# Input projections of a hybrid decoder step: how the first tiles are loaded and split, and when a bias table is spread

## The chip, the cores and the metric

The kernel runs on one core of a Trainium2 chip. The metric is the device time of one execution in microseconds (us). Three runs of the kernel before gave a median of 2597.31 us. The engines are named as in the profile: PE (TensorE matmul; PEld is its weight load), DVE (VectorE), ACT (ScalarE), POOL (GpSimd) and SP (SyncE, which issues most DMAs here). Each works through its own list of instructions in order and waits on semaphores for the others.

## The reference

One layer of a decoder step for a prompt of 2048 positions and for 8 samples of 4 positions, which share the weights. All data is float32.

```python
z = rmsnorm(x, norm1_g) @ w_in            # (2048 + 32) x 1024 @ 1024 x 2560
q, k, v, u, g = split(z, 5)               # 512 columns each
# attention, 8 heads of 64, three dilated branches, relative-position bias, merged
s = q . k / 8 + bias[branch][head, j]     # j: distance 0, d, 2d, ... within the window
# gating: g is layer-normed, multiplied with a causal 128 x 128 matrix per group, times u
x = x + concat(att, u * gate) @ w_out
x = x + (silu(h @ w_gate) * (h @ w_up)) @ w_down      # h = rmsnorm(x, norm2_g), 2816 wide
y = rmsnorm(x, final_g)
```

`rmsnorm` needs the mean of the squares of each row of x. The samples attend over a cache of 2048 keys and values each. The bias is a table lookup by distance; a Toeplitz matrix of it is needed for each head.

## The kernel before

A float32 product is made of three products in a reduced format: each operand is split into a high part (`xh`, `wh`) and a low part (`xl`, `wl`), and PE adds high·high, high·low and low·high (L318 to L320). The high part is a copy on ACT (L135 for x, L220 for weights), the low part a subtraction on DVE or POOL (L138 for x, L226 for weights, on DVE). Lines such as L138 are those of a helper and appear in many places.

The program starts with the input projections, some 600 us, and this is the part that the change touches. The prompt is cut into two halves of 8 tiles of 128 positions, the columns into the five kinds q, k, u, g, v (the second half takes them in the order u, g, q, k, v). For each half and kind there are three groups of tiles, (0, 1, 2), (3, 4, 5) and (6, 7), and for each group eight steps, one for each 128 rows of the contraction. So there are 240 steps, of about 2 us each. In the first half the third group also carries the samples (L323), and their sums are read out of the accumulator by `sample_rows` (L441 on ACT, L442 on DVE).

What runs in which step is written in a planner: `at(step, phase, function, arguments)` notes an event, and `plan.run` sorts them by step, by phase (early, exp, low, scores, turn, mid, values, out, misc, store) and by the order in which they were noted. That order is then the order of the instructions on every engine; nothing is reordered later. An engine may run ahead of the step that PE is in, or fall behind it, as its waits allow.

In the first steps these things run beside the matmuls:

- Columns of the transposed x: tiles 0, 1 and 2 come in halves of 512 rows (`x_half`, L645) into the four `kv` buffers; the other tiles come whole (`x_load`, L198) into one of two `xr` buffers, so that a load has to wait until the tile two before it has been split.
- Rows of x for the norm: `norm1_load` (L239) brings 128 rows into one of two `un` buffers, of which it uses half; `norm1_square` (L243, ACT) squares and sums them. After three, three and two tiles, `norm1_scale` makes the reciprocal roots (L157 on ACT and short DVE instructions). The first output tile of q (`zn`, L330, ACT) needs the first of these; PE then transposes it (L336).
- Weights: eight tiles for each kind (`w_load`, L215, into three `raw` buffers).

Further on in the first half the samples' attention begins. From step 60 on, 96 key units follow each other: a load of cached keys on SP (L519, L523, L526), for some also four new keys (L520) and a broadcast query (`qb`, L531), both issued on ACT's queue from the scratch tensor `zs_d` that SP writes (L449); a multiplication (L537, on DVE or POOL) and a sum (L542, DVE). From step 160 on, the value units run in the same way (loads again on SP; L605 on ACT makes the high part, L611 the low part, L620 and L621 are PE's products).

The bias table is made in steps 50 to 52 (three products, written to the scratch tensors `l12_d` and `l3_d` by L482). In step 55 `table_spread` writes the Toeplitz form to `b_d` with nine DMAs from DRAM to DRAM, eight of 128 runs of 640 elements (L486) and one of 1024 runs of 128 (L488). It is read for the first head in step 228 (L830). After step 240 come attention, the output projection and the feed-forward part; the change does not touch them.

## Time and profile before

| | |
|---|---|
| time, median of 3 runs (lowest, highest) | 2597.31 us (2594.66, 2601.35) |
| the profiled execution's own time | 2594.14 us |
| its span, first to last instruction | 2592.3 us |
| mean granted TensorE clock over the span | 0.985 |
| PE busy, whole span | 2467.8 us, 95% |
| PE busy in the first 600 us | 554.73 us |
| DVE, ACT, POOL busy in the first 600 us | 329.98, 256.67, 219.98 us |
| DMA share in the first 600 us | 0.65 |

How rows of the time line are read: start, duration, engine, line, operation, output<-inputs, shape, count; in brackets the idle time of the engine just before, and after the arrow what ended it. SPq and ACTq are DMA issues on these two queues; their duration is that of the issue, not of the transfer. In the table by stages, each engine has its busy time and, in brackets, its instructions; the last three columns are the granted clock of PE (1.00 is full speed), the busy share of the 16 DMA engines and the rate. PE counts as busy from a matmul's start to its modelled end, so a busy PE is one that does not wait, no more.

### The profile page before, as it was taken

How to read it: one execution, taken by the hardware profiler on the slowest of the kernel's cores; microseconds unless marked ns; L12 is line 12 of the kernel's file. 1: busy time of each engine (PE TensorE's matmuls, PEld its weight loads, DVE VectorE, ACT ScalarE, POOL GpSimd, SP SyncE). 2: the span in 40 equal slices, each digit the busy share in tenths (PEclk: the TensorE clock that was granted, in tenths of full speed). 3: DMA queues.
4: the chain of work that ended last, by engine and by line, in shares of the span. 5: the costliest groups of instructions: out<-in, count | busy, mean ns of one | idle time of the engine just before them, and what ended most of it. 6: DMA issues, size and time to landing. Idle time of an engine off the chain costs nothing.

```text
span 2592.3 us, 38968 instructions
## 1 busy us (share of the span) xinstructions
PE 2467.8 (95%) x13598; PEld 2175.4 (84%) x13598; DVE 1430.4 (55%) x2783; ACT 1221.5 (47%) x2578; POOL 1369.7 (53%) x1068
## 2 busy tenths in 40 slices
PE   8998899999999889999999999999999999999996
PEld 6777776677988768898999988999999987999996
DVE  3359686345888877344444466544444457544445
ACT  5423335446878745554454545432332336444332
POOL 2035654123576745776776743554453634766662
PEclk9999999999999999999999999999999999999998
DMA  7764853588678674464564564455463643755553
GB/s 236 226 204 150 272 159 117 180 247 276 195 223 219 175 210 150 143 206 156 163 195 134 183 187 159 171 187 175 151 215 126 210 154 127 239 194 196 195 195 109
DMA packets 313409, 480.00 MB, mean 185 GB/s; under 512 B 25841, under 2 KB 178834, under 8 KB 307326
## 3 DMA queue, kind: packets, MB, share of 16 engines
q1 hardware_dynamic: 307740, 468.48, 56.7%
q10 hardware_dynamic: 5474, 9.04, 1.3%
q8 instruction: 108, 1.77, 0.3%
q14 instruction: 87, 0.71, 0.1%
HBM read 381.72 MB, written 165.83 MB: 211 GB/s over the span
## 4 chain that ended last, share of the span: by engine, by line
PE 36%; issue 8%; POOL 8%; DMA 4%; ACT 2%; DVE 2%; SPq 1%; POOLq 0%; ACTq 0%; DVEq 0%
PE ps_o L1743 12%; PE ps_m L1665 8%; PE ps_m L1663 8%; PE ps_m L1664 8%; POOL op L1604 2%; DMA ab_d<-pair 2%; ACT fr L1572 1%; POOL pair L1584 1%; POOL dw L138 1%; POOL fr L1587 1%; POOL pair L1593 1%; POOL pair L1590 1%; DMA out_yp_dram<-acc 1%; SPq L1390 1%; PE ps_o L1411 0%
## 5 line engine op out<-in xcount | busy, mean ns | idle before, releaser
L1604 POOL TENSOR_TENSOR op<-fr,op 128x512 fp32r<-128x512 f32 x385 | 488.6, 1298 | 285.1 <-ACT op L1600 273.9
L1665 PE MATMUL ps_m<-xh,op 128*128 128x384 f32 (+5 forms) x1932 | 610.8, 316 | 2.0 <-POOL op L1604 2.0
L1663 PE MATMUL ps_m<-xh,op 128*128 128x384 f32 (+5 forms) x1932 | 610.9, 316 | 0.0
L1664 PE MATMUL ps_m<-xl,op 128*128 128x384 f32 (+5 forms) x1932 | 609.8, 316 | 0.0
L1743 PE MATMUL ps_o<-dw,hw 128*128 128x512 f32 x2040 | 485.8, 393 | 14.8 <-DVE acc L1745 14.8
L1743 PEld LDWEIGHTS ps_o<-dw,hw 128*128 128x128 f32 x2040 | 380.5, 188 | 98.4 <-DVE acc L1745 21.9
L1663 PEld LDWEIGHTS ps_m<-xh,op 128*128 128x128 f32 x1932 | 364.2, 189 | 4.0
L1664 PEld LDWEIGHTS ps_m<-xl,op 128*128 128x128 f32 x1932 | 364.2, 189 | 3.5
L1665 PEld LDWEIGHTS ps_m<-xh,op 128*128 128x128 f32 x1932 | 364.1, 188 | 2.5 <-POOL op L1604 2.5
L1745 DVE TENSOR_TENSOR acc<-acc,ps_o 128x512 f32<-128x512 f32 (+1 forms) x362 | 247.1, 687 | 214.8 <-PE ps_o L1743 214.7
L1710 ACT ACTIVATE ps_t<-zn 128x384 f32<-128x384 f32 (+1 forms) x126 | 58.2, 462 | 463.9 <-DVE zn L1693 364.5
L1600 ACT ACTIVATE op<-fr 128x512 fp32r<-128x512 f32 x396 | 235.5, 623 | 20.8 <-DMA fr<-ab_d 18.1
L138 POOL TENSOR_TENSOR dw<-fd,dw 128x1024 fp32r<-128x1024 f32 x66 | 158.5, 2402 | 120.1 <-ACT dw L135 119.4
L318 PE MATMUL ps_s<-wh,xh 128*128 128x512 f32 x480 | 197.2, 411 | 6.1 <-ACT xh L135 6.0
L319 PE MATMUL ps_s<-wl,xh 128*128 128x512 f32 x480 | 191.7, 399 | 2.0 <-DVE wl L226 2.0
L320 PE MATMUL ps_s<-wh,xl 128*128 128x512 f32 x480 | 191.5, 399 | 0.0
L1604 POOL TENSOR_TENSOR op<-pair,op 128x512 fp32r<-128x512 f32 x63 | 81.2, 1297 | 117.1 <-ACT op L1600 117.1
L1720 ACT ACTIVATE hw<-ps_t 128x384 fp32r<-128x384 f32 (+1 forms) x126 | 56.1, 453 | 175.1 <-DVE ps_t L1716 174.1
L318 PEld LDWEIGHTS ps_s<-wh,xh 128*128 128x128 f32 x480 | 92.5, 193 | 35.9 <-issue 8.4
L319 PEld LDWEIGHTS ps_s<-wl,xh 128*128 128x128 f32 x480 | 92.8, 193 | 20.8 <-DVE wl L226 3.6
L320 PEld LDWEIGHTS ps_s<-wh,xl 128*128 128x128 f32 x480 | 92.2, 192 | 20.4 <-DVE xl L138 0.2
L135 ACT ACTIVATE dw<-fd 128x1024 fp32r<-128x1024 f32 x66 | 69.8, 1057 | 73.1 <-DMA fd<-in_w_down_dram 73.1
(489 smaller groups left out, 4769.6 us busy)
## 6 DMA issues: line engine op xcount, KB each, us to landing
fr<-ab_d SPq DMA_DIRECT2D x308, 256.0 KB
fd<-in_w_down_dram SPq DMA_DIRECT2D x66, 512.0 KB
out_ks_dram<-in_cache_k_dram SPq DMA_DIRECT2D x56, 512.0 KB
out_vs_dram<-in_cache_v_dram SPq DMA_DIRECT2D x56, 512.0 KB
ab_d<-fr SPq DMA_DIRECT2D x88, 256.0 KB
raw<-in_w_in_dram SPq DMA_DIRECT2D x72, 256.0 KB
qk_d<-pair SPq DMA_DIRECT2D x64, 256.0 KB
ab_d<-pair SPq DMA_DIRECT2D x63, 256.0 KB
```

The costliest lines, as they stand in the source:

```text
L135: act.activation(hi, src, AF.Copy)
L138: (eng_lo or pool).tensor_sub(lo, src, hi.bitcast(F32))
L318: pe.matmul(o[j], xh[:, k, :], wh, start=(k == 0), stop=False)
L319: pe.matmul(o[j], xh[:, k, :], wl, start=False, stop=False)
L320: pe.matmul(o[j], xl[:, k, :], wh, start=False, stop=(k == KD - 1))
L1600: act.activation(ops[f, j][0], ab[f][j], AF.Copy)
L1604: (pool if f or j in POOL_LOW else dve).tensor_sub(lo_, ab[f][j], hi.bitcast(F32))
L1663: pe.matmul(out, wh[:, ks], xh[:, :, k], start=(k == 0), stop=False)
L1664: pe.matmul(out, wh[:, ks], xl[:, :, k], start=False, stop=False)
L1665: pe.matmul(out, wl[:, ks], xh[:, :, k], start=False, stop=(k == 3))
L1743: pe.matmul(ps[0:nr], l_, r_[:, cs], start=(z == 0 and y == 0), stop=(z == FC - 1 and y == len(pairs) - 1))
L1745: dve.tensor_add(B.acc[i][0:nr, cs], B.acc[i][0:nr, cs], ps[0:nr])
```

## The change

The change moves work and takes none away. The computed values are the same.

1. Tile 3 of x comes in two halves into the `kv` buffers, like tiles 0 to 2, and POOL subtracts its low parts. Tiles 4 to 7 have the two `xr` buffers to themselves; tiles 4 and 5 are loaded before step 0, 6 in step 3, 7 in step 4; all four are subtracted on DVE (before: 3 and 4 on DVE, 5, 6 and 7 on POOL).
2. For tiles 0 to 7 two row tiles share one `un` buffer, so that four can be under way; their loads, squares and the third scale have new steps. The sample rows are loaded in step 9 (before 13) and split in step 14 (before 15).
3. `table_spread` takes a piece number; the nine pieces stand in steps 186, 188, ... 202 (before: all in step 55).
4. `sample_rows` stands in phase early of a step, one step sooner.

```diff
     def norm1_load(t):
-        xn[t] = quad_tile()[:, 0:2]
+        if t >= KD or t % 2 == 0:
+            xn["two"] = quad_tile()
+        z = t % 2 * 2 if t < KD else 0
+        xn[t] = xn["two"][:, z:z + 2]
         sync.dma_start(xn[t], A["x_prompt"][t * P:(t + 1) * P, :].rearrange("p (a b) -> p a b", a=2))
...
-    def table_spread():
-        for m in range(RUN):
+    def table_spread(m):
+        if m < RUN:
             sync.dma_start(b_d.rearrange("h (r m) c -> m h r c", m=RUN)[m][:, :, 0:640],
                            dap(l12_d, 127 - m * NT, [[768, H], [-1, NT], [1, 640]]))
-        sync.dma_start(b_d[:, :, 640:768], dap(l3_d, 127, [[256, H], [-1, P], [1, P]]))
+        else:
+            sync.dma_start(b_d[:, :, 640:768], dap(l3_d, 127, [[256, H], [-1, P], [1, P]]))
...
-             ("w", 6), ("x", 2, 1), ("w", 7)]
+             ("w", 6), ("x", 2, 1), ("w", 7), ("x", 3, 0), ("x", 3, 1)]
...
-    for t, s0, s1 in ((3, -1, 1), (4, 0, 2), (5, 2, 4), (6, 4, 6), (7, 6, 8)):
+    for t, s0, s1 in ((4, -1, 1), (5, -1, 2), (6, 3, 7), (7, 4, 9)):
         at(s0, "misc", x_load, t)
-        at(s1, "out", x_split, t, pool if t > 4 else dve)
+        at(s1, "out", x_split, t, dve)
...
-    n1 = [(0, 3), (1, 4), (4, 6), (7, 9), (9, 11), (10, 12), (12, 14), (13, 15)] + [(18 + 3 * i, 22 + 3 * i) for i in range(8)]
+    n1 = [(0, 3), (0, 4), (1, 5), (2, 8), (6, 11), (6, 12), (13, 16), (13, 17)] + [(18 + 3 * i, 22 + 3 * i) for i in range(8)]
...
-    at(55, "misc", table_spread)
+    for m in range(RUN + 1):
+        at(186 + 2 * m, "misc", table_spread, m)
...
-                    at(e0 + 6, "out", lambda key=key, kind=kind: sample_rows(kind, outs[key][2]))
+                    at(e0 + 5, "early", lambda key=key, kind=kind: sample_rows(kind, outs[key][2]))
```

PE's list of instructions is the same in both kernels. What changes is the order on the other queues, at three places above all. Line numbers of the changed kernel are three to five higher.

SP at the start, from the first whole tile on; `kv` and `xr` are columns of x, `un` rows, `qk_d` the store of a finished tile. Before:

```order
L198 DMA xr<-in_x_promptT_dram 128x8x128 x2
L239 DMA un<-in_x_prompt_dram 128x1024 x2
L198 DMA xr<-in_x_promptT_dram 128x8x128 x2
L239 DMA un<-in_x_prompt_dram 128x1024
L198 DMA xr<-in_x_promptT_dram 128x8x128
L239 DMA un<-in_x_prompt_dram 128x1024 x4
L347 DMA qk_d<-pair 128x4x128 x2
```

The same place on SP in the changed kernel, from tile 3 on:

```order
L649 DMA kv<-in_x_promptT_dram 128x4x128 x2
L198 DMA xr<-in_x_promptT_dram 128x8x128 x2
L242 DMA un<-in_x_prompt_dram 128x1024 x4
L198 DMA xr<-in_x_promptT_dram 128x8x128 x2
L242 DMA un<-in_x_prompt_dram 128x1024 x2
L293 DMA un<-in_x_sample_dram 32x1024 x2
L295 DMA xr<-in_x_sampleT_dram 128x8x32
L350 DMA qk_d<-pair 128x4x128 x2
```

Tiles 6 and 7 (the second `xr` pair) now stand behind four row tiles instead of being mixed with them, and nothing of the rows stands between the two.

ACT at the same time, from the first whole tiles to the first output tile (L330, in the changed kernel L333); `xh` is a split (L135), `un,ss` a square (L243, now L246). Before:

```order
L243 ACTIVATE un,ss<-un 128x1024
L135 ACTIVATE xh<-xr 128x1024
L243 ACTIVATE un,ss<-un 128x1024
L135 ACTIVATE xh<-xr 128x1024
L243 ACTIVATE un,ss<-un 128x1024
L157 ACT_TABLE_LOAD
L157 ACTIVATE rstd<-rs_vw 128x3
L135 ACTIVATE xh<-xr 128x1024
L243 ACTIVATE un,ss<-un 128x1024
L330 ACTIVATE zn<-ps_s,rstdn 128x512
```

ACT at the same place in the changed kernel:

```order
L135 ACTIVATE xh<-xr 128x1024 x2
L246 ACTIVATE un,ss<-un 128x1024 x3
L157 ACT_TABLE_LOAD
L157 ACTIVATE rstd<-rs_vw 128x3
L135 ACTIVATE xh<-xr 128x1024
L246 ACTIVATE un,ss<-un 128x1024
L135 ACTIVATE xh<-xr 128x1024
L333 ACTIVATE zn<-ps_s,rstdn 128x512
```

Before, the squares alternate with the splits of tiles 4 to 7, and the split of tile 7 and a fourth square stand between the roots and the first output tile. Now the splits of tiles 4 and 5 come first, then three squares and the roots, and the splits of tiles 6 and 7 with a square between them stand ahead of the first output tile.

SP at step 55 before, where the whole spread stands ahead of the write of the sample's keys to `zs_d` and of the first key units' loads:

```order
L493 DMA xr<-in_ohs_dram 33x512 x3
L486 DMA b_d<-l_d 128x1x640 x8
L488 DMA b_d<-l_d 1024x1x128
L449 DMA zs_d<-zn 32x512
L451 DMA out_ks_dram<-zn 8x4x512
L519 DMA kv<-in_cache_k_dram 96x512
L523 DMA kv<-in_cache_k_dram 96x512
L526 DMA kn<-in_cache_k_dram 128x512
```

SP in steps 185 to 190 of the changed kernel, where the first pieces stand now; `kv` are the value units' loads here, `raw` the weights, `cs_d` a finished sample row:

```order
L215 DMA raw<-in_w_in_dram 128x512
L489 DMA b_d<-l_d 128x1x640
L523 DMA kv<-in_cache_v_dram 96x512
L350 DMA qk_d<-pair 128x4x128 x2
L215 DMA raw<-in_w_in_dram 128x512
L523 DMA kv<-in_cache_v_dram 96x512
L215 DMA raw<-in_w_in_dram 128x512
L489 DMA b_d<-l_d 128x1x640
L527 DMA kv<-in_cache_v_dram 96x512
```

The spread no longer stands between the table and the key units; a piece stands ahead of a value load about every second step.

More of the change, by code (lines that the diff above doesn't have):

```diff
@@ L682, in hymba_step @@
         at(b, "misc", norm1_square, t)
-    for s0, a, b in ((7, 0, 3), (13, 3, 6), (16, 6, 8), (46, 8, 16)):
+    for s0, a, b in ((7, 0, 3), (13, 3, 6), (18, 6, 8), (46, 8, 16)):
         at(s0, "early", norm1_scale, a, b)
-    at(13, "misc", sample_load)
-    at(15, "out", sample_split)
+    at(9, "misc", sample_load)
+    at(14, "out", sample_split)
     at(32, "misc", gate_loads)
```

## Prediction

> **What bounds the kernel.** I read the page's busy times first, then the busy times by stages, then PE's time line with the wait ahead of each row, then the queues at the places where PE waits.

> ```profile
> span 2592.3 us, 38968 instructions
> ...
> PE 2467.8 (95%) x13598; PEld 2175.4 (84%) x13598; DVE 1430.4 (55%) x2783; ACT 1221.5 (47%) x2578; POOL 1369.7 (53%) x1068
> ...
> core 0: us, PE busy (x) PEld busy (x) DVE busy (x) ACT busy (x) POOL busy (x), PEclk, DMA share, GB/s
> 0.00:600.00 600.00, 554.73 (x2477) 432.01 (x2478) 329.98 (x585) 256.67 (x428) 219.98 (x153) 0.97 0.65 201
> ...
> 35.00:42.00 7.00, 5.20 (x15) 4.29 (x16) 1.36 (x5) 5.29 (x10) 2.20 (x1) 0.52 0.55 165
> ...
> 180.00:200.00 20.00, 15.47 (x63) 11.54 (x62) 19.90 (x26) 5.41 (x8) 8.89 (x6) 0.97 0.71 198
> ...
> 199.00:202.00 3.00, 3.00 (x8) 2.35 (x8) 2.90 (x7) 0.17 (x2) 0.00 (x0) 0.50 0.47 139
> ```

> PE is the bound. In the first 600 us, the only part that changes, it stands idle 600 − 554.73 = 45.3 us, and it loses more where it runs at a clock near 0.5. PE's list is the same in both kernels, so the change is worth the waits and slow stretches that it removes or adds. The waits it could touch:

> ```profile
> 27.92 0.50 PE L320 MATMUL ps_o<-wh,xl 128*128 128x512 f32 x1 [0.70 <-POOL xl L138]
> ...
> 36.80 1.12 PE L336 MATMUL ps_t<-ident,zn 128*128 128x128 f32 x4 [4.28 <-ACT zn L330]
> ...
> 52.92 0.45 PE L323 MATMUL ps_o<-wh,xs 128*64 128x512 f32 x1 [0.57 <-DVE xs L299]
> ...
> 54.32 0.66 PE L336 MATMUL ps_t<-ident,zn 128*128 128x128 f32 x4 [0.72 <-ACT zn L330]
> ...
> 182.47 0.50 PE L319 MATMUL ps_s<-wl,xh 128*128 128x512 f32 x1 [0.94 <-DVE wl L226]
> ...
> 187.92 0.50 PE L319 MATMUL ps_s<-wl,xh 128*128 128x512 f32 x1 [1.04 <-DVE wl L226]
> ...
> 198.18 0.50 PE L318 MATMUL ps_o<-wh,xh 128*128 128x512 f32 x1 [2.54 <-DVE pair L442]
> ...
> 237.04 0.38 PE L409 MATMUL ps_t<-vnh,wg_h 128*128 128x256 f32 x1 [2.14 <-DVE un L417]
> ...
> 270.79 1.88 PE L459 MATMUL ps_t<-pair,wbd 32*32 32x64 f32 x16 [3.90 <-issue]
> ...
> 327.43 0.80 PE L318 MATMUL ps_o<-wh,xh 128*128 128x512 f32 x1 [8.05 <-DVE zn L442]
> ...
> 480.77 0.42 PE L620 MATMUL ps_t<-vh,z 128*64 128x512 f32 x1 [3.90 <-DVE z L591]
> ```

> The execution shown took 2594.14 us, its span and 1.8 us around it, and is 3.2 us under the median of the runs, 2597.31. I make the sum against the former and take it off the median.

> **A. Loads and splits at the head.**

> ```profile
> 17.49 1.06 ACT L135 ACTIVATE xh<-xr 128x1024 fp32r<-128x1024 f32 x1 [1.27 <-DMA xr<-in_x_promptT_dram]
> ...
> 19.51 1.06 ACT L135 ACTIVATE xh<-xr 128x1024 fp32r<-128x1024 f32 x1 [0.96 <-DMA xr<-in_x_promptT_dram]
> ...
> 19.84 2.40 SPq L198 DMA_DIRECT2D xr<-in_x_promptT_dram  x2
> ...
> 20.61 1.23 DVE L138 TENSOR_TENSOR xl<-xr,xh 128x1024 fp32r<-128x1024 f32 x1 [0.80 <-ACT xh L135]
> ...
> 20.79 1.06 ACT L243 ACTIVATE un<-un 128x1024 f32<-128x1024 f32 x1 [0.22 <-DMA un<-in_x_prompt_dram]
> ...
> 24.34 1.06 ACT L135 ACTIVATE xh<-xr 128x1024 fp32r<-128x1024 f32 x1 [2.40 <-DMA xr<-in_x_promptT_dram]
> ...
> 25.47 2.39 POOL L138 TENSOR_TENSOR xl<-xr,xh 128x1024 fp32r<-128x1024 f32 x1 [8.72 <-ACT xh L135]
> ...
> 27.89 0.37 SPq L198 DMA_DIRECT2D xr<-in_x_promptT_dram  x1
> ...
> 33.71 1.06 ACT L135 ACTIVATE xh<-xr 128x1024 fp32r<-128x1024 f32 x1 [1.71 <-DMA xr<-in_x_promptT_dram]
> ...
> 35.02 1.06 ACT L243 ACTIVATE un<-un 128x1024 f32<-128x1024 f32 x1 [0.26 <-DMA un<-in_x_prompt_dram]
> ...
> 36.08 0.67 ACT L330 ACTIVATE zn<-ps_s,rstdn 128x512 f32<-128x512 f32 x1
> ```

> The wait of 4.28 is a chain. Tile 7's load stands on SP until POOL has subtracted tile 5 (25.47 + 2.39 = 27.86; issue at 27.89), lands at 33.71, and its split and a square stand ahead of `zn` on ACT, which ends at 36.75. In the changed kernel tile 5's load no longer waits for a buffer. Column tiles in a backlog land 19.51 − 17.49 = 2.02 us apart, a row tile after a column tile 20.79 − 19.51 = 1.28. Tile 4 then lands at 19.5, tile 5 at 21.5 (24.34 before), four row tiles at 22.8, 24.1, 25.4 and 26.6. Tile 6's load waits only for tile 4's subtraction, now on DVE (19.5 + 1.06 + 1.23 = 21.8, inside the backlog), and lands at 28.7; tile 7's at 30.7, or up to 1.3 later, since it took 5.8 from issue to split (27.89 to 33.71) where tile 5 took 4.5 (19.84 to 24.34). Split 1.06, `zn` 0.67: ready at 32.4 to 33.7. PE has reached its transposes at 36.80 − 4.28 = 32.5, or 31.8 without the wait of 0.70 before, so 0.6 to 1.9 us of wait remain. I take 1.3, which gains 3.0. The half clock in 35 to 42 costs 5.20 × 0.48 = 2.5 us of running; with a short wait left I take half, 1.2. The 0.70 goes, because tile 5's low part is ready at 21.5 + 1.06 + 1.23 = 23.8. The 0.57 and 0.72 go, with the sample rows issued four steps earlier and the squares ahead of time: 1.3. Sum 6.2, between 0 (tile 7 as late as before) and 0.70 + 4.28 + 2.5 + 0.57 + 0.72 = 8.8.

> The subtractions of tiles 5 to 7 leave POOL (2.4 each) for DVE (1.23 each), which is busy 1.36 of 7 us here; POOL's two halves of tile 3 fall in its idle 8.72. The new waits on SP (a row tile for the squares of the pair before, stores behind the sample rows) delay only what is needed later: nothing taken; if that cover goes, a row tile is 1.3 late.

> [...]

> **B. The spread leaves step 55.**

> ```profile
> 136.11 5.48 SPq L486 DMA_DIRECT2D b_d<-l_d  x8
> ...
> 141.64 0.64 SPq L488 DMA_DIRECT2D b_d<-l_d  x1
> ...
> 142.37 10.40 SPq L449 DMA_DIRECT2D zs_d<-zn  x1
> ...
> 152.05 0.26 DVE L501 COPY bias_s<-ps_t 128x96 f32<-128x96 f32 x1 [17.47 <-PE ps_t L500]
> ...
> 153.58 0.44 SPq L519 DMA_DIRECT2D kv<-in_cache_k_dram  x1
> ...
> 156.72 0.69 ACT L399 ACTIVATE un<-ps_s,rstd 128x512 f32<-128x512 f32 x1 [15.59 <-DMA zs_d<-zn]
> ...
> 161.62 0.69 DVE L537 TENSOR_TENSOR pr<-kv,qb 100x512 f32<-100x512 f32 x1 [9.31 <-DMA qb<-zs_d]
> ```

> The nine DMAs hold SP from 136.11; the write of `zs_d` behind them takes 10.40 us to issue, ACT waits 15.59 for it, and the first key product on DVE starts at 161.62 after 9.31 us of idleness. DVE is then behind: busy 19.90 of 20 us in 180 to 200, and PE waits for it at 182.47, 187.92 and 198.18. Without the nine, `zs_d` is issued at 136.1 instead of 152.77, so the query comes 16.7 earlier, at 144.9, and the first key product follows DVE's copy at 152.3: 9.3 us earlier. DVE's backlog of key sums is of that size, so the three waits go: 0.94 + 1.04 + 2.54 = 4.5, and with them the half clock in 199 to 202 (3.00 × 0.50 = 1.5). Gain 6.0, between 0 and 6.0. The waits at 237.04, 270.79 and 480.77 I leave: behind 202 the units have caught up, and these name other work.

> **C. The samples' sums a step earlier.**

> ```profile
> 326.04 0.69 DVE L542 TENSOR_REDUCE S_s<-pr 100x8 f32<-100x512 f32 x1
> ...
> 326.64 0.73 DVE L442 SCALAR_TENSOR_TENSOR zn<-ps_o,rstds,zn 32x512 f32<-32x512 f32 x1
> ```

> L442 moves ahead of one key sum only. In the wait of 8.05 at 327.43 that sum stands right ahead of it, so 0.6 goes (326.64 − 326.04), of 0 to 0.7.

> **D. The nine pieces among the value loads.** Each stands on SP ahead of one; `b_d` is read from step 228 on, long behind step 202, so nobody waits for the pieces themselves.

> ```profile
> 474.17 0.33 SPq L519 DMA_DIRECT2D kv<-in_cache_v_dram  x1
> ...
> 481.23 0.63 ACT L605 ACTIVATE vh<-kv 100x512 fp32r<-100x512 f32 x1 [0.21 <-PE ps_t L620]
> ```

> A piece can delay what is behind it by 0 to (152.77 − 136.11) / 9 = 1.85 us, all nine by 0 to 16.7; a gain is excluded, as nothing waits for less traffic. The load issued at 474.17 is used 7.06 us later, and ACT then waited for PE, not for the load. That cover is nearly four times 1.85; I take 1.0 for all. If the cover were gone, the upper end.

> **Sum.** 6.2 + 6.0 + 0.6 − 1.0 = 11.8: the profiled execution would go from 2594.1 to 2582.3, the median to 2585.5. By the bounds of the terms alone: 8.8 + 6.0 + 0.7 = 15.5 gained (2581.8) to 16.7 lost (2614.0).

> **Rivals.**
> 1. The head gains nothing: tile 7 stands behind four row tiles and lands as late as now. For it: its 5.8 us from issue to split are DMA, not waiting. Against it: its issue comes some 4 us sooner. Gain 6.0 + 0.6 − 1.0 = 5.6: 2591.7.
> 2. DVE's backlog is its own load, 19.90 of 20, and an earlier start only lets it wait earlier. Against it: the units start 9.3 us late and PE's waits end once that is made up. Gain 6.2 + 0.6 − 1.0 = 5.8: 2591.5.
> 3. Slower: the pieces delay the value units, whose products are in PE's list, so PE stands. At 1.85 a piece 12.8 − 16.7 = −3.9: 2601.2; with a half-clock stretch of 1.5 after every second piece 2608. The gain is eaten from 12.8 / 9 = 1.4 us a piece. Against it: the cover of 7 us. [...]
> 4. An earlier start also clears the waits at 237.04 and 270.79: 6.0 more, 2579.5, or 2576.5 with their clock. Against it: they name the norm of the gates and an issue.

> **How the numbers follow.** Forecast 0.51 (its own range 2578 to 2590, for A's remaining wait and D's price), rival 1 0.13, rival 2 0.08, rival 3 0.18, rival 4 0.10. Runs differ by some 0.3%, 7.8 us, which is about what a measurement of this kernel can tell from no change: faster is under 2589.5, slower over 2605.1. Faster: 0.46 of the forecast and rival 4, 0.56. Same: 0.05 of the forecast, rivals 1 and 2, and rival 3's cheap end, 0.29. Slower: the rest, 0.15. The range 2574 to 2602 takes in rivals 1, 2 and 4 and rival 3's cheap end.

> **What would show it.** A: `zn` starts near 32 to 33 and PE's wait ahead of its first transposes is under 2 us. B: the write of `zs_d` is issued near 136, the first key product starts near 152, no PE wait over 0.5 in 180 to 200, clock 1.0 there. C: the 8.05 at 327 is some 0.6 shorter. D: no new PE wait on a value load between 465 and 515. I would be wrong if PE's wait at the head stays over 3 us, if key units start early and PE still waits for DVE, or if value units wait for `kv`.

## The result and the profile after

The changed kernel is faster. In the first comparison its median was 2574.16 us (4 runs, 2571.27 to 2577.57) against 2597.26 us before: a ratio of 0.991, 95% interval 0.9891 to 0.9929, which is 23.1 us. Two later comparisons, with more runs, gave less: 0.9945 (0.9929 to 0.9960, 14.9 us between the medians) and 0.9941 (0.9926 to 0.9956, 13.9 us). The forecast was 11.8, and 2574.16 lies under its own range of 2578 to 2590.

The profiled execution took 2577.57 us against 2594.14, so the two traces differ by 16.6 us. The page and the table by stages, as before:

```profile
span 2575.8 us, 38969 instructions
...
PE 2462.4 (96%) x13598; PEld 2175.2 (84%) x13598; DVE 1435.6 (56%) x2785; ACT 1222.9 (47%) x2579; POOL 1365.4 (53%) x1067
...
0.00:600.00 600.00, 564.30 (x2549) 441.46 (x2550) 342.81 (x608) 266.14 (x452) 220.77 (x157) 0.98 0.67 207
...
35.00:42.00 7.00, 7.00 (x35) 5.75 (x34) 3.53 (x16) 4.17 (x10) 0.00 (x0) 1.00 0.91 270
...
180.00:200.00 20.00, 20.00 (x90) 16.54 (x90) 19.21 (x41) 5.59 (x11) 8.50 (x6) 1.00 0.41 128
```

PE's idle time in the first 600 us went from 45.3 to 35.7 us. In 35 to 42 it now runs throughout at full clock (5.20 of 7 at 0.52 before), and in 180 to 200 too (15.47 of 20), although DVE is as full there as it was. PE's time line, its waits of more than 3 us in the first 600 after the first product:

```profile
221.59 0.38 PE L412 MATMUL ps_t<-vnh,wg_h 128*128 128x256 f32 x1 [3.60 <-DVE un L420]
...
255.69 1.05 PE L462 MATMUL ps_t<-pair,wbd 32*32 32x64 f32 x16 [3.54 <-issue]
...
302.77 0.50 PE L322 MATMUL ps_s<-wl,xh 128*128 128x512 f32 x1 [3.10 <-DVE wl L226]
...
312.29 0.79 PE L321 MATMUL ps_o<-wh,xh 128*128 128x512 f32 x1 [6.04 <-DVE zn L445]
...
465.17 0.64 PE L624 MATMUL ps_t<-vh,z 128*64 128x512 f32 x1 [3.86 <-DVE z L595]
```

The waits at the head and the three in 180 to 200 are gone. Those behind 220 stay with other lengths (2.14, 3.90, 8.05 and 3.90 before; 3.60, 3.54, 6.04 and 3.86 now), and one of 3.10 at 302.77 is new.

The table shows where the time is, in us from the start of PE's first product of one step to that of another, worked out from the rows of PE in each profile. It holds for one execution of each kernel.

| kernel | 0 to 8 | 8 to 20 | 60 to 64 | 72 to 84 | 84 to 184 | 184 to 220 |
|---|---|---|---|---|---|---|
| before | 19.3 | 35.6 | 8.3 | 32.0 | 258.2 | 97.5 |
| changed | 21.1 | 26.0 | 9.9 | 24.5 | 256.2 | 97.8 |
| changed, e13_after | 20.2 | 27.2 | 9.9 | 24.5 | 255.9 | 98.0 |
| e1_head | 19.4 | 28.2 | 9.9 | 27.7 | 258.7 | 97.5 |
| e2_spread | 18.8 | 34.5 | 11.1 | 24.5 | 255.9 | 98.3 |
| e3_rows | 19.5 | 35.1 | 9.7 | 26.6 | 261.8 | 98.6 |
| e6_block | 19.3 | 26.3 | 8.3 | 24.5 | 256.2 | 113.3 |
| e7_early | 21.0 | 27.9 | 9.9 | 24.5 | 259.6 | 98.3 |
| e8_pool | 20.6 | 26.0 | 8.3 | 24.5 | 253.7 | 97.8 |
| e9_nopair | 20.7 | 32.6 | 8.3 | 24.5 | 255.8 | 97.6 |
| e11_twofold | 20.0 | 26.0 | 8.3 | 24.5 | 255.3 | 102.2 |
| e12_small | 20.8 | 26.0 | 8.3 | 24.5 | 255.5 | 97.5 |

In the first two rows, the changed kernel is 9.6 shorter between steps 8 and 20 and 1.8 longer ahead of them; steps 72 to 84 are 7.5 shorter; the steps with the nine pieces are 0.4 longer. Steps 184 to 220 take 97.5 to 98.6 in the four profiles that have no piece there, so a cost of 0.4 can't be told from none.

### The profile page after: what moved, and what is told of

Its sections match the earlier page's. It is cut to its first block, busy times and chain, and to the rows that moved or that the text cites. A ratio compares the mean times of both kernels' runs of the same rounds, so it can differ in the third digit from the quotient of the medians.

```text
span 2575.8 us, 38969 instructions
## 1 busy us (share of the span) xinstructions
PE 2462.4 (96%) x13598; PEld 2175.2 (84%) x13598; DVE 1435.6 (56%) x2785; ACT 1222.9 (47%) x2579; POOL 1365.4 (53%) x1067
## 5 line engine op out<-in xcount | busy, mean ns | idle before, releaser
L138 POOL TENSOR_TENSOR dw<-fd,dw 128x1024 fp32r<-128x1024 f32 x66 | 158.7, 2405 | 118.7 <-ACT dw L135 118.5
L323 PE MATMUL ps_s<-wh,xl 128*128 128x512 f32 x480 | 191.3, 398 | 0.0
L323 PEld LDWEIGHTS ps_s<-wh,xl 128*128 128x128 f32 x480 | 92.4, 192 | 20.5 <-DVE xl L138 0.2
L615 POOL TENSOR_TENSOR vl<-kv,vh 100x512 fp32r<-100x512 f32 (+1 forms) x32 | 46.2, 1446 | 109.8 <-ACT vh L609 40.1
```

The source lines that it names most:

```text
L138: (eng_lo or pool).tensor_sub(lo, src, hi.bitcast(F32))
L323: pe.matmul(o[j], xl[:, k, :], wh, start=False, stop=(k == KD - 1))
```

## Experiments

The theory to be tested: head and spread each give some 6 to 9 us, they add, the sums of the samples give nothing, and the pieces cost nothing because they stand apart. The rivals: one of the two gives nearly all; the gain is the later place and not the spacing; the subtraction on DVE, or the order of the loads alone, made the head's gain.

### The three parts alone

Each is the kernel before with one part of the change's diff: for e1_head the loads, splits and rows, for e2_spread `table_spread`, for e3_rows `sample_rows`. e4_after is the changed kernel beside them.

```diff
# e2_spread (table_spread takes a piece number as in the change)
...
-    at(55, "misc", table_spread)
+    for m in range(RUN + 1):
+        at(186 + 2 * m, "misc", table_spread, m)
# e3_rows
-                    at(e0 + 6, "out", lambda key=key, kind=kind: sample_rows(kind, outs[key][2]))
+                    at(e0 + 5, "early", lambda key=key, kind=kind: sample_rows(kind, outs[key][2]))
```

> The kernel before with the head alone changed: loads, splits, rows in pairs, sample rows earlier. The forecast's term A: 6.2 us faster than before. By the traces of before and after, in which PE is 7.6 us ahead at step 20: 7.6 faster. If the head also clears waits after step 60, more than 10. If the head's gain is only the spread's shown earlier, under 2. In its profile the wait at 36.80 is gone, and the nine transfers still hold the write of zs_d for some 10 us.

> The kernel before with the spread alone moved to steps 186 to 202. Terms B and D of the forecast: 6.0 - 1.0 = 5.0 faster. By the traces: 5.9 between steps 60 and 84, some 1.9 more up to step 96, 0.4 lost in steps 184 to 220, so 7.4. If the medians' gap of 23 us is mostly the spread's, 12 or more.

> The kernel before with sample_rows alone a step earlier. Term C: 0.6 faster, which is below what can be told from none (within 2 us of before). If the copy of the accumulators frees PE earlier in every kind (five times), up to 5 faster, and PE's waits on pair or zn of the samples' sums are shorter in its profile.

> The changed kernel again, for its median: the profiles differ by 16.6 us, the medians by 23.1. If the profiled pair shows the change truly and the medians are chance, the gap is near 17 now; if not, 20 or more. The sum of the three parts alone against this gap tells whether the parts add.

| | median | before | ratio (95% interval) |
|---|---|---|---|
| e1_head | 2586.46 | 2593.61 | 0.9975 (0.9965 to 0.9985) |
| e2_spread | 2584.45 | 2593.61 | 0.9965 (0.9952 to 0.9978) |
| e3_rows | 2593.10 | 2593.61 | 1.0002 (0.9992 to 1.0013) |
| e4_after | 2578.72 | 2593.61 | 0.9945 (0.9929 to 0.9960) |

By the ratios the head alone gives 6.5 us, the spread alone 9.1, the sums −0.5: together 15.1, against 14.3 for the whole on the same chip. The parts add. By the medians the spread is the larger one, but the intervals, 3.9 to 9.1 for the head and 5.7 to 12.4 for the spread, overlap. That one part gives nearly all is out.

In the profile of e3_rows a gain is handed back. PE's time line in it:

```profile
195.74 0.50 PE L318 MATMUL ps_o<-wh,xh 128*128 128x512 f32 x1 [1.69 <-DVE pair L442]
...
226.00 0.39 PE L409 MATMUL ps_t<-vnh,wg_h 128*128 128x256 f32 x1 [4.08 <-ACT vnh L135]
```

The waits of 0.94 and 1.04 are absent, the third is 1.69 instead of 2.54, and steps 72 to 84 take 26.6 instead of 32.0. But the wait at 226 is 4.08 instead of 0.82, and steps 84 to 184 take 3.6 more. One profile doesn't show that this is the work of `sample_rows`: e1_head, which leaves it where it was, lacks the first two waits as well and takes 27.7 for steps 72 to 84.

### The size, and the sums in their place

e13_after is the changed kernel a third time, e14_norows the changed kernel with `sample_rows` where it was.

```diff
# e14_norows
-                    at(e0 + 5, "early", lambda key=key, kind=kind: sample_rows(kind, outs[key][2]))
+                    at(e0 + 6, "out", lambda key=key, kind=kind: sample_rows(kind, outs[key][2]))
```

> The changed kernel a third time. The first comparison (4 runs of each) gave 23.1 us, the second (6 runs against 25 on another chip) 14.9, the two profiles 16.6. If the size is some 15, the ratio is 0.993 to 0.996; if the first was right, under 0.9925.

> The changed kernel with sample_rows back in its old step: term C in its place. Forecast of C: 0.6 slower than the changed kernel, within 1.5 us of it. If head and spread need it (DVE later at the samples' sums), 3 us slower or more, and PE's wait behind 300 is longer than in the changed kernel.

e13_after: 2578.07 against 2591.94, ratio 0.9941 (0.9926 to 0.9956). e14_norows: 2576.17, ratio 0.9943 (0.9925 to 0.9961). The size is some 14 to 15 us; the 23.1 of the first comparison were not seen again, and why its four runs of each lay so far apart stays open (its two profiled executions differ by 16.6, 15.2 of it by step 236). `sample_rows` changes nothing that can be measured, alone or with the rest.

### The pieces: place, spacing, number

```diff
# e6_block: all nine in one step
-        at(186 + 2 * m, "misc", table_spread, m)
+        at(186, "misc", table_spread, m)
# e7_early: apart, among the key loads
-        at(186 + 2 * m, "misc", table_spread, m)
+        at(55 + 2 * m, "misc", table_spread, m)
# e5_double: each twice, into the same tensor
         at(186 + 2 * m, "misc", table_spread, m)
+        at(186 + 2 * m, "misc", table_spread, m)
# e11_twofold: each twice, the second into a scratch tensor c_d of its own
+    c_d = dram.tile([H, P, 768], F32, name="c_d")
...
-    def table_spread(m):
+    def table_spread(m, b_d=b_d):
...
         at(186 + 2 * m, "misc", table_spread, m)
+        at(186 + 2 * m, "misc", table_spread, m, c_d)
```

> The changed kernel with all nine pieces in step 186: is it the later place or the pieces apart that gains. If the place alone does it (nothing there waits for the write behind them), as fast as the changed kernel within 2 us. If a block of nine holds SP there too, for some 10 to 17 us as before, less the 7 us of cover of a value load: 3 to 10 us slower than the changed kernel, with a PE wait on a value product behind 460.

> The changed kernel with the nine pieces one at a time in steps 55, 57, ... 71, among the key units' loads. If only the block ahead of the write of zs_d mattered, zs_d is issued near 129, the first key product starts near 145 and the time is that of the changed kernel within 2 us. If key loads behind the pieces come late (1.85 us a piece), DVE falls behind again by up to 16 us and 5 to 9 us of the gain are lost, with PE waits on DVE before 200.

> The changed kernel with each of the nine pieces issued twice (same contents): prices D. Forecast of D: nine pieces cost 1.0, so 1.0 slower than the changed kernel, some 14 us faster than before. By the traces of before and after, 0.4 between steps 184 and 220: 0.4 slower. Rival 3 at 1.85 a piece uncovered: 16.7 slower, which is no faster than before.

> The changed kernel with nine more pieces, each beside one of the nine, into a scratch tensor of its own that nobody reads. The run with the pieces twice into the same tensor was 32 us slower, but there the second issue of each pair stood until the first had landed (5.5 to 8 us for the two). Without that wait: if a piece apart costs next to nothing, 0 to 2 us slower than the changed kernel; at 1.85 a piece, 16.7 slower; if two in a row already hold SP as the nine did, 5 to 15 slower, with issues of more than 2 us behind the pairs.

| | median | before | ratio (95% interval) |
|---|---|---|---|
| e6_block | 2594.11 | 2592.83 | 1.0008 (0.9996 to 1.0020) |
| e7_early | 2582.20 | 2592.83 | 0.9957 (0.9941 to 0.9973) |
| e5_double | 2611.30 | 2592.83 | 1.0068 (1.0052 to 1.0083) |
| e11_twofold | 2580.31 | 2591.51 | 0.9958 (0.9945 to 0.9971) |

The block in the late place loses the whole gain. SP's queue, ACT and PE in e6_block:

```profile
455.36 5.50 SPq L489 DMA_DIRECT2D b_d<-l_d  x8
460.90 1.18 SPq L492 DMA_DIRECT2D b_d<-l_d  x1
462.18 9.28 SPq L523 DMA_DIRECT2D kv<-in_cache_v_dram  x1
...
475.19 0.63 ACT L609 ACTIVATE vh<-kv 100x512 fp32r<-100x512 f32 x1 [8.60 <-DMA kv<-in_cache_v_dram]
...
466.36 0.66 PE L624 MATMUL ps_t<-vh,z 128*64 128x512 f32 x1 [8.12 <-DVE z L595]
479.90 1.86 PE L633 MATMUL ps_o<-om,sel 64*4 64x512 f32 x2 [7.55 <-DVE pair L345]
```

The value load behind the nine takes 9.28 us to issue, where the write of `zs_d` took 10.40 before (8.97 in e1_head, 9.25 in e3_rows): it isn't that write, but what stands behind the nine. ACT waits 8.60 for the value load and PE's two waits are 8.12 and 7.55 (3.90 for one of them in the kernel before). Steps 184 to 220 take 113.3 instead of 97.8.

In the changed kernel, and even with two in a row in e11_twofold, the issues are short for the first eight pieces, of 128 runs each. SP's queue of the changed kernel, with the ninth piece (1024 runs, L492) in the last two rows, then that of e11_twofold:

```profile
458.39 0.71 SPq L489 DMA_DIRECT2D b_d<-l_d  x1
459.20 0.41 SPq L523 DMA_DIRECT2D kv<-in_cache_v_dram  x1
...
466.77 0.66 SPq L489 DMA_DIRECT2D b_d<-l_d  x1
467.52 0.41 SPq L527 DMA_DIRECT2D kv<-in_cache_v_dram  x1
...
499.87 0.65 SPq L492 DMA_DIRECT2D b_d<-l_d  x1
501.11 4.37 SPq L530 DMA_DIRECT2D kv<-in_cache_v_dram  x1
```

```profile
454.76 0.72 SPq L490 DMA_DIRECT2D b_d<-l_d  x1
455.53 0.65 SPq L490 DMA_DIRECT2D c_d<-l_d  x1
456.27 0.40 SPq L524 DMA_DIRECT2D kv<-in_cache_v_dram  x1
```

The ninth piece holds the load behind it even alone: 4.37 us here, 3.1 to 4.5 in the ten profiles that have it apart. So a part of the block's 9 to 10 us belongs to this one transfer, and how the rest divides among the other eight was not tested. PE does not wait for it: in the changed kernel it stands idle 0.00 us in steps 200 to 212.

Nine more pieces cost 4.3 us in the steps where they stand (102.2 against 97.8), 3.0 of them behind step 200, where the second ninth piece takes 4.72 to issue and the load behind it 2.96. The ratio of 0.9958 against the changed kernel's 0.9945 and 0.9941 makes it 3 to 4, with intervals that overlap. In e5_double the same number of transfers cost 32 us. It differs from e11_twofold only in that the second of a pair writes what the first writes, and the two issues then take 5.84 us instead of 0.72 + 0.65, because SP waits for the first transfer, as its list of waits says (5.61 to 7.99 us for the two issues in the nine pairs). SP's queue of e5_double:

```profile
458.25 5.84 SPq L489 DMA_DIRECT2D b_d<-l_d  x2
464.18 0.41 SPq L523 DMA_DIRECT2D kv<-in_cache_v_dram  x1
```

Held 5.6 to 8.0 us at a time, nine times, SP brings the value loads late one after the other, and the 7 us ahead of a single load don't cover it. That run priced a held queue, not a piece.

e7_early keeps a part of the gain with the pieces apart in the early place. Steps 72 to 84 take 24.5, as in the changed kernel, but steps 84 to 184 take 259.6, where the twelve profiles with the spread in the late steps take 253.7 to 256.9. By the ratios it gains 11.1 us, the changed kernel 14 to 15, and e1_head, which has the head and the block in the early place, 6.5. So spacing gives some 4.6 of the spread's 8 us without the later place, and the later place some 3 to 4 more; the traces show this order, but the intervals of the medians overlap. The later place without the spacing gives nothing (e6_block).

### The head's parts

```diff
# e8_pool: tiles 5, 6 and 7 subtracted on POOL again
-        at(s1, "out", x_split, t, dve)
+        at(s1, "out", x_split, t, pool if t > 4 else dve)
# e9_nopair: a buffer for each row tile again
-        if t >= KD or t % 2 == 0:
-            xn["two"] = quad_tile()
-        z = t % 2 * 2 if t < KD else 0
-        xn[t] = xn["two"][:, z:z + 2]
+        xn[t] = quad_tile()[:, 0:2]
```

> The changed kernel with the subtractions of tiles 5, 6 and 7 on POOL again (2.4 us each instead of 1.23): the part of the head that frees tile 7's buffer sooner. In the changed kernel tile 5 is subtracted from 23.38 to 24.61; on POOL to some 25.8, so tile 7's load is issued 1.2 later, inside the backlog of four row tiles: tile 7 lands no later, the first output tile still near 32, and the time is that of the changed kernel within 2 us. If the subtraction is what counted in the chain of 4.28, a wait of 1 to 3 us comes back ahead of the first transposes, with a stretch at half clock: 2 to 5 us slower.

> The changed kernel with each row tile in a buffer of its own again, so that two and not four can be under way; everything else as changed. SP then holds the third row tile, and with it tiles 6 and 7, until the first square is done (24.6 in the changed kernel), the fourth until the second (25.9). If the free buffers made the gain, tile 7 lands 3 to 5 us later, the wait ahead of the first transposes is back with 2 to 4 us and its half clock, and the kernel is 3 to 6 us slower than the changed one. If the order of the loads alone made it, within 2 us.

e8_pool: 2579.46 against 2591.51, ratio 0.9959 (0.9945 to 0.9973); steps 8 to 20 take 26.0, as in the changed kernel. The engine that subtracts is not what counted. e9_nopair: 2581.95, ratio 0.9966 (0.9955 to 0.9978); steps 8 to 20 take 32.6. The medians alone (2.5 us between the two) wouldn't settle it; the trace of e9_nopair shows the wait back:

```profile
15.40 9.51 SPq L239 DMA_DIRECT2D un<-in_x_prompt_dram  x4
25.01 1.77 SPq L198 DMA_DIRECT2D xr<-in_x_promptT_dram  x2
...
34.16 1.06 ACT L135 ACTIVATE xh<-xr 128x1024 fp32r<-128x1024 f32 x1 [4.58 <-DMA xr<-in_x_promptT_dram]
...
37.83 1.02 PE L336 MATMUL ps_t<-ident,zn 128*128 128x128 f32 x4 [4.81 <-ACT zn L330]
```

The same rows of the changed kernel:

```profile
15.82 3.69 SPq L242 DMA_DIRECT2D un<-in_x_prompt_dram  x4
22.85 2.16 SPq L198 DMA_DIRECT2D xr<-in_x_promptT_dram  x2
...
29.22 1.06 ACT L135 ACTIVATE xh<-xr 128x1024 fp32r<-128x1024 f32 x1 [0.44 <-DMA xr<-in_x_promptT_dram]
31.23 1.04 ACT L135 ACTIVATE xh<-xr 128x1024 fp32r<-128x1024 f32 x1
32.18 0.67 ACT L333 ACTIVATE zn<-ps_s,rstdn 128x512 f32<-128x512 f32 x1
```

Without the paired buffers four row loads hold SP for 9.51 us, tiles 6 and 7 are issued 2.2 later, the first of them is split at 34.16 instead of 29.22, and PE waits 4.81. From the issue of the two to that split it is 9.2 us instead of 6.4; why the load itself also takes longer was not looked into. So the order of the loads needs the free buffers.

### The small products ahead of the key units

In several profiles PE runs slowly at step 60 with no wait ahead of it. The time line and the table by stages there, for the changed kernel:

```profile
141.52 2.84 PE L504 MATMUL ps_t<-rb,xr 33*128 33x8 f32 x24
144.30 0.78 PE L321 MATMUL ps_s<-wh,xh 128*128 128x512 f32 x1
...
144.00:147.00 3.00, 3.00 (x10) 2.42 (x10) 2.56 (x5) 0.00 (x0) 0.35 (x1) 0.56 0.22 70
```

Behind 24 products of 8 columns the granted clock is 0.56 over these 3 us: 0.50 from 144.34 on. e10_small, e12_small and e15_small are one kernel: the changed one with these products in three parts.

```diff
-        for a in range(3):
-            for t in range(ST):
+        for t in range(ST):
...
-    at(60, "turn", sample_table)
+    for a in range(3):
+        at(58 + a, "turn", sample_table, a)
```

> The changed kernel with the 24 small products of the sample table (8 columns each, 3.3 us in a row on PE at step 60) in three parts, in steps 58, 59 and 60. In five of the six profiles so far PE runs 2 to 6 us at a clock of 0.5 to 0.6 right behind them with no wait ahead, and steps 60 to 64 take 9.5 to 11.1 us instead of 8.2. If the stretch of small products is what lowers the clock, this window goes and 1.5 to 2.5 us are gained; if it is chance or an earlier cause, the window stays and the time is that of the changed kernel.

> The changed kernel with the sample table's small products in three parts again, for a profile that can be read: one execution before it took 8602 us, with PE at a third of its pace from end to end, and it was the profiled one. If the stretch of small products lowers the clock, steps 60 to 64 take 8.2 us and the granted clock is 1.00 there; 1 to 2.5 us faster than the changed kernel. If not, the window is there in most runs and the time is the same.

> The changed kernel with the small products in three parts, against the changed kernel on the same chip. If the window at half clock behind them costs what the profiles show, 1.5 to 2.5 us faster than the changed kernel, and no clock under 0.9 between steps 60 and 64; if other windows take its place, the same time.

Ratios: 0.9936 (0.9920 to 0.9951), 0.9942 (0.9929 to 0.9955) and 0.9937 (0.9923 to 0.9952); e15_small has 2576.42 against 2578.07 for the changed kernel on the same chip. One execution of e10_small, the profiled one, took 8602 us with PE at a third of its pace from end to end; its profile is not used. In e12_small the clock stays:

```profile
143.00:147.00 4.00, 4.00 (x22) 3.19 (x21) 2.02 (x5) 0.00 (x0) 0.00 (x0) 1.00 0.05 10
```

In both readable profiles with three parts steps 60 to 64 take 8.3 us, and steps 56 to 60 take 0.6 more. With the products in a row the slow stretch stands in 9 of 14 profiles (9.7 to 11.1 us for the four steps) and is absent in 5, the kernel before among them. Two profiles alone would not prove the theory, but where the products stand settles it. In every profile the granted clock changes only at the edges of windows of 3.41 us (the last section works this out), and these edges lie elsewhere against the products each time. In the 9 profiles with the slow stretch, the window ahead of it holds 1.99 to 2.84 us of the small products; in the 5 without it an edge divides them and no window holds more than 2.00, and with three parts 1.21. The changed kernel, cut at these edges:

```profile
140.93:144.34 3.41, 3.41 (x28) 3.00 (x27) 0.00 (x0) 0.00 (x0) 0.00 (x0) 1.00 0.29 94
144.34:147.75 3.41, 3.41 (x9) 2.74 (x9) 3.31 (x6) 0.00 (x0) 1.10 (x1) 0.50 0.37 119
```

The slow stretch costs 1.6 us in steps 60 to 64. The time of the whole is not told apart from that of the changed kernel.

## Why the forecast was right in direction and short in size

The likeliest case and its mechanism held: both groups of waits go, and the pieces cost next to nothing. The sum, 11.8, was short against the 14 to 15 of the larger comparisons, and half of the first one's 23.1. The step that failed is the size of B, which counted the three listed waits and one half-clock stretch of one execution where the backlog cost 8 us; A was short by about 1. Why the first comparison gave 8 more than the others stays open. Term by term:

**A, the head: 6.2, and 6.5 by e1_head alone.** The chain of landings came out: tile 6 was to land at 28.7 and is split at 29.22, `zn` was to be ready at 32.4 to 33.7 and is issued at 32.18 and done at 32.85. In the step "so 0.6 to 1.9 us of wait remain. I take 1.3", the wait was about right and the half of the clock's loss that was left behind it was not. In the twelve profiles with the new loads and the paired buffers PE's idle time in steps 8 to 20 is 0 to 2.0 us, none in five of them, the changed kernel's among these, and the granted clock never falls there. Steps 0 to 20 take 45.7 to 48.9 in the twelve and 53.3 to 54.8 in the three profiles with the head of before, 7.3 between the means.

Steps 0 to 8 are 1.8 longer in the changed kernel's profile. That comes from the moment when PE's pace doubles after its first products, and not from POOL's work. PE before, then in the changed kernel:

```profile
10.41 0.63 PE L320 MATMUL ps_s<-wh,xl 128*128 128x512 f32 x1
...
11.18 0.40 PE L319 MATMUL ps_s<-wl,xh 128*128 128x512 f32 x1
```

```profile
13.79 0.63 PE L321 MATMUL ps_s<-wh,xh 128*128 128x512 f32 x1
...
14.88 0.39 PE L321 MATMUL ps_s<-wh,xh 128*128 128x512 f32 x1
```

Products start 0.43 us apart at first and 0.23 apart later; the trace records full clock from 11.07 on before and from 14.63 on in the changed kernel. In the sixteen profiles that moment lies between 10.16 and 14.63 and the length of steps 0 to 8 follows it: less half of the moment, 13.4 to 13.9 us remain in all of them. e1_head and e6_block, with the new head, reach it at 12.09 and 11.44 and take 19.4 and 19.3, as the kernel before does. The moment is 11.44 to 14.63 in the thirteen profiles with the new loads and 10.16 to 11.58 in the three without; whether the change makes it later on the average is open with three. So the step "POOL's two halves of tile 3 fall in its idle" cost PE nothing, though DVE takes longer beside them. DVE and POOL, before and then changed:

```profile
13.76 4.20 DVE L226 SCALAR_TENSOR_TENSOR wl<-w,g1c,wh 128x512 fp32r<-128x512 f32 x3
15.45 1.30 POOL L138 TENSOR_TENSOR xl<-kv,xh 128x512 fp32r<-128x512 f32 x1 [0.45 <-ACT xh L135]
```

```profile
14.05 5.22 DVE L226 SCALAR_TENSOR_TENSOR wl<-w,g1c,wh 128x512 fp32r<-128x512 f32 x3
15.49 1.52 POOL L138 TENSOR_TENSOR xl<-kv,xh 128x512 fp32r<-128x512 f32 x1 [0.17 <-ACT xh L135]
17.24 3.16 POOL L138 TENSOR_TENSOR xl<-kv,xh 128x512 fp32r<-128x512 f32 x2 [0.23 <-ACT xh L135]
```

With one more subtraction on POOL beside them, DVE's three subtractions of weights take 5.22 instead of 4.20 (5.19 in e1_head and 5.27 in e4_after, which have the same loads); in e14_norows, where POOL starts its next subtraction only at 17.91, they take 4.15. What makes them longer is not shown. PE does not wait for these low parts. Its wait of 0.41 at 8.15 is for a high part of weights on ACT and is 0 to 0.58 in the other profiles with this head; its cause wasn't looked into. Rival 1, tile 7 no earlier, is out: that is what e9_nopair shows when the buffers are not free.

**B, the spread: 6.0, and 7.5 in steps 72 to 84 of the trace.** The places came out: PE starts step 60 at 144.30 instead of 151.94, and as far ahead of the forecast places, 136.1 and 152.3, stand the write of `zs_d` and the first key product. SP and DVE of the changed kernel:

```profile
128.48 0.31 SPq L452 DMA_DIRECT2D zs_d<-zn  x1
...
144.40 0.26 DVE L505 COPY bias_s<-ps_t 128x96 f32<-128x96 f32 x1 [17.46 <-PE ps_t L504]
144.58 0.68 DVE L541 TENSOR_TENSOR pr<-kv,qb 100x512 f32<-100x512 f32 x1
```

The first key product follows DVE's copy. The step "so the three waits go", with 4.5 for them and 1.5 for the half clock, was too small in two ways. Steps 72 to 84 went from 32.0 to 24.5, where 4.5 of listed waits and 1.7 for 3.41 us at half clock make 6.2. The other 1.3 is time in which PE counts as busy. For one, the product ahead of the wait of 0.94 starts 1.34 before the one behind it (181.13 and 182.47), where products otherwise start 0.23 apart, so that wait cost 1.11 and not 0.94, and the product behind it holds the next one back by another 0.1 (182.47 to 182.81, 0.34 apart). And the gain doesn't end at step 84. From step 64 to 184 the three profiles with the block in step 55 take 300.9 to 304.7 and the twelve with the spread in the late steps 292.7 to 295.9, 8.0 between the means. This is the mis-sized term: B and D were to give 5.0, and e2_spread alone gives 9.1 (5.7 to 12.4). Rival 2, that DVE's backlog is its own load, was half true and harmless: DVE is busy 19.21 of 20 us in 180 to 200, but ahead of PE.

**C: 0.6, and nothing.** The order moved by one key sum as said, but the wait at 308 to 327 is 3.4 to 9.4 us long from one kernel to the next, with this part (3.4 in e9_nopair, 8.2 in e8_pool) and without it (5.2 in e14_norows, 9.4 in e2_spread), so 0.6 of it can't be seen.

**D: 1.0, and 0.4 in the trace, which can't be told from nothing.** The range up to 16.7 was the price of a block, as e6_block shows (15.4), not of pieces apart. Rival 3 did not come, for two reasons of which I gave one: an issue behind one of the first eight pieces takes 0.33 to 0.82 in the changed kernel, where the piece stands alone, and behind the ninth, where it takes 4.37, the cover held.

**Behind step 84**, where I left all waits, 2.1 us went: rival 4 in part. The waits there changed their places and lengths rather than vanished.

## What to carry to other kernels

Price a row of transfers from DRAM to DRAM by how long the next issue behind it stands; the cure here was to set them apart. As a block the nine held the issue behind them for 10.40 us in the early place and for 9.28 in the late one; set apart in the changed kernel, the eight of 128 runs left it at 0.33 to 0.82, and only the one of 1024 runs held it, for 4.37. Take the gain of a removed backlog from the length of the whole stage against one without it, not from the sum of the waits that are long enough to be listed. A load that was reordered to come early needs a free buffer to be early (tile 6 is split at 29.22 with the paired buffers, at 34.16 without). Work given to an idle engine can go with a slower neighbour (DVE's three subtractions took 5.22 us instead of 4.20 when POOL had one more), which is worth asking about only where somebody waits for that neighbour. Before a difference of 1 to 2 us between two profiles is put down to the change, look where the clock changed in each.

## What was not expected of the hardware

So the same wait costs the clock in one execution and not in another. The wait of 2.54 ahead of 198.18 before lies in one window (195.4 to 198.8), and half clock follows; a wait of 2.54 ahead of 190.30 in e1_head is divided into 1.82 and 0.72, and the clock stays full. By these windows, and as an estimate, the half clock behind a wait of some 2 to 4 us is a matter of chance, and a longer one (over 2 x 1.94 = 3.9) brings it wherever the edge falls.

Why half clock follows the small products, with 1.99 to 2.84 us of them in the window ahead and PE never idle in it, is not shown here.
